# Attention ends shared out anew between VectorE and GpSimd, B's heads first in the output projection, and maxima that end a slot earlier, in a fused hybrid attention step

## The chip, the core and the metric

The kernel runs on one core of a Trainium2 chip. The metric is the device time of one execution in microseconds (us). The core's engines each run their own queue of instructions in order: TensorE (PE; its weight loads are PEld), VectorE (DVE), ScalarE (ACT), GpSimd (POOL) and SyncE (SP), which only issues DMAs here. They wait for one another by semaphores.

## What is computed

One layer of a diffusion backbone with two mixers, A (global attention, 8 query heads on 2 key heads) and B (attention in a window of 128 on either side, with a learned sink logit). There are 1024 latent tokens and 128 prompt tokens. Cut to what matters:

```python
h = rmsnorm(x, norm_gain) * (1.0 + scale) + shift           # adaLN
q_a, k_a, v_a, g_a, q_b, k_b, v_b, g_b = project(h, w_in)   # q and k normed, latents rotated
o_a = softmax(q_a @ [k_ctx, k_a].T / 8) @ [v_ctx, v_a]      # latents: all 9 blocks of 128 keys
o_b = softmax([sink, q_b @ [k_ctx, band(k_b)].T / 8])[1:] @ [v_ctx, band(v_b)]
x = x + gate * (concat(o_a * silu(g_a), o_b * silu(g_b)) @ w_out)
```

The prompt's tokens go through the same weights and attend to the prompt alone (one block of keys). All arithmetic is float32; products that need it are split into a high and a low part.

## The kernel before

The first 300 us make the modulation, the normed tokens, the projections (queries and gates go to DRAM, keys and values stay on the chip) and the gates. Then comes the attention, to which all of the change belongs.

**Units and slots.** A unit is (t, m, g): a tile t of 128 tokens, a mixer m (0 is A, 1 is B) and a group g of 4 heads. The units go t = 1 to 8, and for each t: A and B of group 0, then A and B of group 1; the prompt (t = 0) has the last four, units 32 to 35. A unit takes one slot for each of its key blocks: A 9, B 4 (3 for t = 1 and t = 8), a prompt unit 1, padded to 2. A pair of A and B thus has 13 slots. All engines' instructions are written out by one loop over slots, and the order that it gives is kept on each engine. A slot does this, in this order: what was put off to it by `later(n, f)` (f is run n slots on); the scores of its block (`scores`, st, and their exponentials pe); what `put` has entered for the slot in advance (maxima, B's weights); a share of the output projection from a queue `outq` (2 products a slot, 4 in the prompt); and, two slots after a unit's last block, its products with the values (`values`).

**A's softmax** uses a maximum over all keys, found beforehand: `max_items` makes 12 products pmx (L932) and as many reductions on VectorE (L933) in the 13 slots ahead of the unit. Its `finish` loads qb (the low part of the queries) and reduces the 12 maxima to m_nat (L943, L946); TURN slots later `transpose` lets TensorE turn m_nat to rows (ptm, L951) and VectorE multiply them into qb (L952), which the scores' second product (L1207) reads. `finish` stands at `start[i] - MX_LEAD` for latents and at `start[i] - LEAD` for the prompt; LEAD is 4 and does not change. Units 0 and 2 get theirs ahead of the loop, and for them, too, `transpose` comes TURN slots after `finish`.

**PSUM** is eight banks: A has two (pmx, ptm, B's first scores sn, and pti, a small transpose for B), B two (st), C two (pv, the products with the values), D and E one each (po, the output projection). A product that goes to a bank waits until its former content has been read.

**The end of a unit** (in `values`): T is the slot with the unit's last products. ENDS gives for A and B how many slots after T the steps come. For A: `inverse` at T+1 (ScalarE: rs, the reciprocals of the sums, as exp(-ln)), GpSimd's multiplication of the loaded gate sgl by rs at T+2 (L1248), `gated` at T+3 (VectorE: of = pv times sgl, L1254; it is written to the tile spare or of), `parts` at T+4 (ScalarE: the high part ogh, L1264) and T+5 (the low part ogl, L1267: GpSimd, or VectorE for units 30 and 31). B has its sums in earlier and steps at T+1 to T+4. At T+6 `out_items` puts the 24 products of the pair into `outq`: for each half of the columns, four 64-row pieces k of w_out in the order KS, and three products for each.

```python
MX_LEAD = 3
TURN = 2
ENDS = ((1, 3, 4), (1, 2, 3, 6))
KS = (0, 1, 4, 5, 2, 3, 6, 7)     # 0 to 3: A's heads, 4 to 7: B's; first four: group 0
```

On the prompt's last slots the scores of B are turned and normalised by VectorE (pen, L1030) before TensorE takes them (L1202); that needs the sums, which GpSimd completes (L1025).

Of the kernel before, what the change touches and what calls it, by code (L numbers as in the profile page):

```python
# [9 lines left out]
F32 = mybir.dt.float32  # L10
F32R = mybir.dt.float32r
BF16 = mybir.dt.bfloat16
AF = mybir.ActivationFunctionType
ALU = mybir.AluOpType
# [4 lines left out]
P = 128  # L19
# [12 lines left out]
CKV = {0: 512, 1: 1792}  # L32
WRAW = 3
PROMPT_AT = 32
KS = (0, 1, 4, 5, 2, 3, 6, 7)
PL_DVE = (4,)
LAG = 2
LEAD = 4
# [5 lines left out]
NAT_FIRST = (0, 1, 2, 3)  # L44
MX_AT = (-4, -3, -2, -2, -1, 4, 5, 5, 7, 7, 8, 8)
MX_FIRST = (0, 1, 2, 3, 3, 4, 4, 5, 6, 7, 7, 8)
MX_LEAD = 3
LAST_END = (1, 3, 5, 7)
SPLIT_LAG = 2

# [7 lines left out]
WO_LATE = {12: 9, 13: 10, 11: 21, 15: 21, 14: 24}  # L58

WO_STEPS = ((0, 4, 4), (1, 5, 5), (2, 6), (3, 7), (4, 8, 6), (5, 9), (6, 11), (7, 12, 10), (8, 12), (9, 13), (10, 14))  # L60
TURN = 2
QUERY_AT = (0, 2, 3, 6)
PAD = 2
X_FROM = 2
# [14 lines left out]
PES = 12  # L79
SPLIT = 6  # L80
GATE_LATE = 2
ENDS = ((1, 3, 4), (1, 2, 3, 6))
QTS = 5
PROMPT_LEAD = 4
PROMPT_PV = "CCAC"
# [45 lines left out]
def hybrid_step(ctx, tc, x_prompt, x_sample, cache_k_a, cache_v_a, cache_k_b, cache_v_b,  # L131
# [3 lines left out]
    nc = tc.nc  # L135
# [14 lines left out]
    def later(n, f):  # L150

        agenda.setdefault(now[0] + n, []).append(f)

    def tick():
        now[0] += 1
        for f in agenda.pop(now[0], ()):
            f()
# [8 lines left out]
    def bank(tag, name):  # L166
        return ps.tile([P, 512], F32, tag=tag, name=name, bufs=BANKS[tag])
# [174 lines left out]
    with tc.tile_pool(name="st", bufs=2, side="right") as st:  # L342
# [136 lines left out]
        for j in range(KT + 2):  # L479
# [79 lines left out]
            if KT - 2 <= j < KT:  # L559
# [3 lines left out]
                c0, n = W_QA.cols[0]  # L563
# [50 lines left out]
    with tc.tile_pool(name="qt", bufs=2, side="right") as qt:  # L614
# [108 lines left out]
        for m in range(2):  # L723
            w, nxt = ((W_QA, W_QB), (W_QB, W_KV))[m]
            ts = list(range(1, NT)) + [0]
            for t in ts:
# [3 lines left out]
                if (m, t) in ((0, ts[-2]), (1, ts[GATE_AT[0]])):  # L730
                    n = len(wg) // 2
# [171 lines left out]
    qtile, qbtile, mxtile, sgl = {}, {}, {}, {}  # L903
# [11 lines left out]
    def max_items(i):  # L915
# [19 lines left out]
        def finish():  # L935
# [10 lines left out]
            nc.vector.tensor_scalar(mn, m4, -1.0, None, op0=ALU.mult)  # L946
            later(TURN, transpose)

# [170 lines left out]
    for f in beside[2]:  # L1119
# [5 lines left out]
        name=nc.get_next_instruction_name(), engine=mybir.EngineType.Activation, act_func_set_id=6))  # L1125
# [3 lines left out]
    w2 = ctx.enter_context(tc.tile_pool(name="w2", bufs=2, side="right"))  # L1129
# [54 lines left out]
    def load_gate(i):  # L1184
        if i < NU:
            t, m, g = units[i]
            sgl[i] = w2.tile([P, 2, P], F32, tag="sgl", name=f"sgl{i}", bufs=4)
            h0 = HD * (8 * m + 4 * g)
            nc.sync.dma_start(
                sgl[i], g_dram[h0 : h0 + 4 * HD, P * place(t) : P * place(t) + P].rearrange("(c p) n -> p c n", p=P))  # L1190
# [27 lines left out]
    def values(i, made, first, last):  # L1218

        t, m, g = units[i]  # L1220
        if first:
            pvb[i] = bank("C", f"pv{i}")
        pv = pvb[i]

        def product(o, lhs, rhs, start, stop):
            r = rhs.rearrange("p (c s n) -> p c s n", s=2, n=P)
            for s in range(2):
                nc.tensor.matmul(pv[HD * s : HD * s + HD, o : o + 256].rearrange("p (c n) -> p c n", c=2), lhs,  # L1228
                                 r[:, :, s, :], start=start, stop=stop)

        n = len(made)
        for b, (blk, pe) in enumerate(made):
            product(0, blk[1], pe, first and b == 0, m == 1 and b == n - 1)
        if not last:
            return
        if m == 0:
            product(256, ones, acc.pop(i), False, True)

        v = {}

        def inverse():
            if m == 1:
                return
            rs = w2.tile([P, 256], F32, tag="rs", name=f"rs{i}")
            nc.scalar.activation(rs, pv[:, 256:512], AF.Ln)
            nc.scalar.activation(rs, rs, AF.Exp, scale=-1.0)
            sg = sgl[i]
            later(1, lambda: nc.gpsimd.tensor_tensor(sg, sg, rs.rearrange("p (c n) -> p c n", c=2), op=ALU.mult))  # L1248

        def gated():  # L1250
            o = 768 + 256 * (i % 4)
            of = spare[0][:, o : o + 256] if i % 4 < 3 else w2.tile([P, 256], F32, tag="of", name=f"of{i}", bufs=1)
            of = of.rearrange("p (c n) -> p c n", c=2)
            nc.vector.tensor_tensor(of, pv[:, 0:256].rearrange("p (c n) -> p c n", c=2), sgl.pop(i), op=ALU.mult)  # L1254
            later(GATE_LATE, lambda: load_gate(i + 4))
            v["of"] = of

        def parts():
            while held[0] == NOG:
                outq.pop(0)()  # L1260
            held[0] += 1
            oh = ogp.tile([P, 2, P], F32R, tag="ogh", name=f"ogh{i}")
            ol = ogp.tile([P, 2, P], F32R, tag="ogl", name=f"ogl{i}")
            nc.scalar.copy(oh, v["of"])  # L1264
            og[t, 2 * m + g] = oh, ol
            eng = nc.vector if i - PROMPT_AT in LOW_DVE else nc.gpsimd
            later(1, lambda: eng.tensor_tensor(ol, v["of"], oh, op=ALU.subtract))  # L1267

        for n, f in zip(ENDS[m], (inverse, gated, parts)):
            later(n, f)  # L1270
        if m == 1:
            later(ENDS[m][3], lambda: outq.extend(out_items(t, g)))

# [12 lines left out]
    def out_items(t, g):  # L1286

        last = t == units[-1][0]


        pieces = ((0, 512, "D"), (512, 768, "E"), (768, 1024, "C")) if last else ((0, 512, "D"), (512, 1024, "E"))

        def mm(c, k, p):

            a, b, tag = pieces[c]
            n = a // 512
            q = slice(a - 512 * n, b - 512 * n)
            if k == KS[0] and p == 0:
                po[c] = bank(tag, f"po{t}_{c}")[:, 0 : b - a]
            if c == 0 and k == KS[4] and p == 0:  # L1300
                for j in range(2):
                    load_sum(t, j)
            oh, ol = (x[:, k % 2, :] for x in og[t, k // 2])
            x, lo = ((oh, 0), (oh, 1), (ol, 0))[p]
            nc.tensor.matmul(po[c], x, wo_parts[KT * n + k][lo][:, q], start=(k == KS[0] and p == 0),  # L1305
                             stop=(k == KS[-1] and p == 2))
            if b == D and k % 2 == 1 and p == 2:
                held[0] -= 1
            if k == KS[-1] and p == 2:
                nc.vector.tensor_tensor(po[c], po[c], gt[n][:, q], op=ALU.mult)  # L1310
                nc.vector.tensor_tensor(yt[n][:, q], po[c], yt[n][:, q], op=ALU.add)
                nc.sync.dma_start(y_tile[t][:, a:b], yt[n][:, q])

        ks = KS[4 * g : 4 * g + 4]
        return [lambda c=c, k=k, p=p: mm(c, k, p) for c in range(len(pieces)) for k in ks for p in range(3)]
# [13 lines left out]
    for i, (t, m, g) in enumerate(units):  # L1329
        if i in EARLY:  # L1330
            continue
        if m == 0:
            items, done = max_items(i)
            at, end = [start[i - 2] + a for a in (MX_AT if i > 2 else MX_FIRST)], start[i] - MX_LEAD
            if t == 0:
# [19 lines left out]
    for i in range(4):  # L1355
        load_gate(i)
    for s in range(len(slots) + LAG + ENDS[1][3]):
        tick()
        if s < len(slots) and slots[s]:
            i, b, last, blk = slots[s]  # L1360
# [86 lines left out]
```

## Time and profile before

| | |
|---|---|
| time, median of 3 runs | 695.03 us (693.94 to 695.07) |
| the profiled execution | 694.89 us, its span 693.0 us |
| busy: TensorE, VectorE, GpSimd, ScalarE | 97%, 54%, 47%, 45% of the span |
| mean granted TensorE clock | 0.994 of full speed |
| 13 slots (a pair) in the middle of the attention | 22.7 us |

The span runs from the first to the last instruction; the rest of the execution's time lies around it. A row of the timeline gives the start, the duration, the engine, the source line, the operation, the tiles (written, then read), how many instructions the row joins, and in brackets how long the engine had been idle and what ended that. Of an engine that is busy 97% of the time, only its own idle time and what lengthens it count.

### The profile page before, as it was taken

The numbers are of one execution on the slowest core, as the hardware profiler recorded it, in microseconds if no ns is written. First come the engines' busy times: TensorE is split into PE (matmuls) and PEld (weight loads), VectorE is DVE, ScalarE is ACT, GpSimd is POOL, SyncE is SP. The second block draws the span as 40 slices with busy tenths as digits, with TensorE's granted clock in tenths as the row PEclk, the third lists the DMA queues.
The fourth block names the chain that finished last, engine by engine and source line by source line (L and its number), as shares of the span: only waits on it lengthen the run. The fifth ranks groups of instructions, "written<-read, shape, count | busy, mean of one in ns | idle before, by whom it ended". The sixth has DMA issues, their size and how long they took to land.

```text
span 693.0 us, 10923 instructions
## 1 busy us (share of the span) xinstructions
PE 675.0 (97%) x3896; PEld 522.8 (75%) x3896; DVE 374.3 (54%) x857; ACT 309.0 (45%) x692; POOL 323.3 (47%) x340
## 2 busy tenths in 40 slices
PE   6999999999999999998999999999999999999997
PEld 3688988878788788985667777777777777777666
DVE  3565237875684772535446455455455563645343
ACT  4555411412243452456445445555456445545450
POOL 3466023332322140657575457545664566446730
PEclk9999999999999999999899999999999999999999
DMA  8960283339436015533122122212221212112323
GB/s 339 413 255 21 109 303 77 78 92 285 133 88 191 8 62 161 165 105 108 58 82 71 54 85 68 92 54 69 70 84 47 91 61 78 55 55 68 122 61 122
DMA packets 53446, 78.65 MB, mean 113 GB/s; under 512 B 6848, under 2 KB 25728, under 8 KB 52368
## 3 DMA queue, kind: packets, MB, share of 16 engines
q1 hardware_dynamic: 45360, 66.28, 28.4%
q10 hardware_dynamic: 8032, 11.68, 6.3%
q8 instruction: 31, 0.51, 0.3%
q14 instruction: 23, 0.19, 0.1%
HBM read 58.72 MB, written 19.21 MB: 112 GB/s over the span
## 4 chain that ended last, share of the span: by engine, by line
PE 87%; DMA 4%; DVE 3%; ACT 2%; issue 1%; POOL 1%; ACTq 1%; SPq 1%; DVEq 0%; POOLq 0%
PE pv L1228 14%; PE po L1305 14%; PE st L1206 5%; PE pmx L932 5%; PE st L1207 4%; PE pq L279 4%; PE pq L280 4%; PE pq L278 4%; PE st L1202 4%; PE pg L288 3%; PE pg L292 3%; PE pg L293 3%; PE pk L279 2%; PE pk L280 2%; PE pk L278 2%; DMA wm<-in_w_mod_ss_dram 2%
## 5 line engine op out<-in xcount | busy, mean ns | idle before, releaser
L1215 POOL TENSOR_TENSOR acc<-acc,pe 128x512 f32<-128x512 f32 x112 | 143.5, 1281 | 37.8 <-ACT pe L1208 35.4
L933 DVE TENSOR_REDUCE mx<-pmx 128x1 f32<-128x384 f32 x192 | 101.7, 554 | 103.8 <-PE pmx L932 101.5
L1208 ACT ACTIVATE pe<-st 128x512 f32<-128x512 f32 x146 | 85.4, 596 | 89.8 <-PE st L1207 89.6
L1228 PE MATMUL pv<-pe,v_all 128*64 128x256 f32 x832 | 101.6, 387 | 0.0
L1228 PEld LDWEIGHTS pv<-pe,v_all 128*64 128x64 f32 x832 | 57.3, 138 | 38.3 <-issue 8.4
L993 DVE CUSTOM_DVE_ANT_0 sn<-sn,mask,nsink 128x512 f32<-128x512 f32 (+1 forms) x64 | 46.3, 724 | 68.6 <-PE sn L990 67.9
L1305 PE MATMUL po<-wo,ogh 128*128 128x512 f32 (+1 forms) x224 | 75.8, 390 | 0.0
L197 POOL TENSOR_TENSOR rs_q<-ms_q,mhalf 128x8 f32<-128x8 f32 x18 | 34.8, 1931 | 80.8 <-DVE ms_q L195 80.8
L932 PE MATMUL pmx<-kha,qt 128*128 128x384 f32 x192 | 63.3, 376 | 3.7 <-ACT pen L979 3.1
L1215 POOL TENSOR_TENSOR acc<-pe,pe 128x512 f32<-128x512 f32 x16 | 20.4, 1276 | 96.2 <-ACT pe L1208 73.9
L1206 PE MATMUL st<-qt,kha 128*128 128x512 f32 x144 | 61.4, 426 | 1.2 <-ACT pe L1208 1.1
L979 ACT ACTIVATE pen<-sn,nm 128x512 f32<-128x512 f32 (+2 forms) x72 | 45.3, 631 | 31.4 <-DVE nm L993 28.6
L1207 PE MATMUL st<-qb,kla 68*128 68x512 f32 x144 | 57.2, 397 | 0.0
L1203 ACT COPY pe<-st 128x512 f32<-128x512 f32 x62 | 36.4, 587 | 32.9 <-PE st L1202 32.9
L932 PEld LDWEIGHTS pmx<-kha,qt 128*128 128x128 f32 x192 | 34.9, 192 | 12.8 <-ACT pen L979 7.7
L1305 PEld LDWEIGHTS po<-wo,ogh 128*128 128x128 f32 x224 | 41.5, 190 | 3.5
L1305 PE MATMUL po<-wo,ogl 128*128 128x512 f32 (+1 forms) x112 | 43.6, 389 | 0.0
L1206 PEld LDWEIGHTS st<-qt,kha 128*128 128x128 f32 x144 | 27.2, 189 | 20.9 <-issue 8.5
L1202 PE MATMUL st<-ident_r,pen 128*128 128x128 f32 x248 | 37.5, 274 | 1.1 <-DVE pen L1030 1.1
L441 POOL TENSOR_TENSOR h<-hf,h 128x256 fp32r<-128x256 f32 (+2 forms) x33 | 28.0, 862 | 20.7 <-DVE h L440 20.7
L1202 PEld LDWEIGHTS st<-ident_r,pen 128*128 128x128 f32 x248 | 29.2, 141 | 7.5 <-ACT ogh L1264 1.5
L675 ACT ACTIVATE sqq<-pq 128x512 f32<-128x512 f32 x18 | 10.8, 599 | 53.3 <-DMA qd<-qo0q 15.6
(235 smaller groups left out, 1506.9 us busy)
## 6 DMA issues: line engine op xcount, KB each, us to landing
qt<-qd SPq DMA_DIRECT2D x36, 256.0 KB
wm<-in_w_mod_ss_dram SPq DMA_DIRECT2D x8, 1024.0 KB
qd<-qo0q ACTq DMA_DIRECT2D x36, 128.0 KB
qd<-qo1q ACTq DMA_DIRECT2D x36, 128.0 KB
sgl<-gd SPq DMA_DIRECT2D x36, 128.0 KB
out_dram<-yt SPq DMA_DIRECT2D x17, 256.0 KB
xn<-in_x_sample_dram SPq DMA_DIRECT2D x8, 512.0 KB
wg<-in_w_mod_g_dram SPq DMA_DIRECT2D x4, 1024.0 KB
```

The lines of the kernel that those rows point to most:

```text
L278: nc.tensor.matmul(out, h_at(0, i, k, tok), w.hi[k], start=(k == 0), stop=False)
L932: nc.tensor.matmul(pm[:, 0:384], lhs, kha[:, g, 3 * b : 3 * b + 3, :], start=True, stop=True)
L933: nc.vector.tensor_reduce(mx[:, h, b : b + 1], pm[:, 0:384], axis=AX.X, op=ALU.max)
L979: nc.scalar.activation(penat[i][:, h], s, AF.Exp, bias=v["nm"][:, h : h + 1], scale=scale, accum_out=v["sum"][:, h : h + 1])
L993: nc.vector.tensor_tensor_reduce(s, s, mask[:, m0 : m0 + n], -1.0, nsink[:, 4 * g + h : 4 * g + h + 1], op0=ALU.add, op1=ALU.min, accum_ou ...
L1202: nc.tensor.transpose(s[:, P * h : P * h + P], penat[i][:, h, o : o + P], ident_r.bitcast(F32))
L1206: nc.tensor.matmul(s, kh, qtile[i], start=True, stop=False)
L1207: nc.tensor.matmul(s, kl, qbtile[i], start=False, stop=True)
L1208: nc.scalar.activation(pe, s, AF.Exp)
L1215: nc.gpsimd.tensor_tensor(acc[i], first, pe, op=ALU.add)
L1228: nc.tensor.matmul(pv[HD * s : HD * s + HD, o : o + 256].rearrange("p (c n) -> p c n", c=2), lhs, r[:, :, s, :], start=start, stop=stop)
L1305: nc.tensor.matmul(po[c], x, wo_parts[KT * n + k][lo][:, q], start=(k == KS[0] and p == 0), stop=(k == KS[-1] and p == 2))
```

## The change

Five edits. (1) VectorE multiplies A's values by rs instead of by the gate, and GpSimd, right behind that in the same slot (T+3), multiplies the product by the gate; its multiplication at T+2 is gone. For B nothing changes. (2) `parts` for A comes at T+5 instead of T+4, so that the low part comes at T+6. (3) KS puts B's heads ahead of A's within each group. (4) MX_LEAD is 4 instead of 3: `finish` of a latent unit stands a slot earlier. (5) TURN is 3 instead of 2: `transpose` comes three slots after `finish`, so that it stays where it was for latents from unit 4 on, and comes one slot later for units 0 and 2 and for the prompt's units 32 and 34.

```diff
-KS = (0, 1, 4, 5, 2, 3, 6, 7)
+KS = (4, 5, 0, 1, 6, 7, 2, 3)
...
-MX_LEAD = 3
+MX_LEAD = 4
...
-TURN = 2
+TURN = 3
...
-ENDS = ((1, 3, 4), (1, 2, 3, 6))
+ENDS = ((1, 3, 5), (1, 2, 3, 6))
...
-            rs = w2.tile([P, 256], F32, tag="rs", name=f"rs{i}")
-            nc.scalar.activation(rs, pv[:, 256:512], AF.Ln)
-            nc.scalar.activation(rs, rs, AF.Exp, scale=-1.0)
-            sg = sgl[i]
-            later(1, lambda: nc.gpsimd.tensor_tensor(sg, sg, rs.rearrange("p (c n) -> p c n", c=2), op=ALU.mult))
+            v["rs"] = w2.tile([P, 256], F32, tag="rs", name=f"rs{i}")
+            nc.scalar.activation(v["rs"], pv[:, 256:512], AF.Ln)
+            nc.scalar.activation(v["rs"], v["rs"], AF.Exp, scale=-1.0)
...
-            nc.vector.tensor_tensor(of, pv[:, 0:256].rearrange("p (c n) -> p c n", c=2), sgl.pop(i), op=ALU.mult)
+            sg = sgl.pop(i)
+            by = sg if m else v["rs"].rearrange("p (c n) -> p c n", c=2)
+            nc.vector.tensor_tensor(of, pv[:, 0:256].rearrange("p (c n) -> p c n", c=2), by, op=ALU.mult)
+            if m == 0:
+                nc.gpsimd.tensor_tensor(of, of, sg, op=ALU.mult)
```

On TensorE, at the first two slots of the attention (st_0 and st_1 are unit 0's scores, sn_0 unit 1's; pg_late are products of the gates that are fitted in), there stands before:

```order
L951 MATMUL ptm_3392<-ident_r,m_nat_110 4x128
L1206 MATMUL st_0_3395<-qt_2991,kha 128x512
L1207 MATMUL st_0_3395<-qb_3181,kla 128x512
L989 MATMUL sn_0_3405<-khb,qt_2993 128x384
L990 MATMUL sn_0_3405<-klb,qt_2993 128x384
```

and after the change, from the last two of the six late products on:

```order
L1137 MATMUL pg_late<-h_2_0_140,late_ogl_2984 128x384
L1137 MATMUL pg_late<-h_2_0_142,late_ogh_2980 128x384
L951 MATMUL ptm_3412<-ident_r,m_nat_110 4x128
L1206 MATMUL st_1_3416<-qt_2991,kha 128x512
L1207 MATMUL st_1_3416<-qb_3181,kla 128x512
L989 MATMUL sn_1_3423<-khb,qt_2993 128x384
```

Unit 2's turn, ptm, has moved from ahead of slot 0 to ahead of slot 1, where sn_1 follows two products later; ptm and sn_1 have the same one of A's two banks, as they had before.

On TensorE in the prompt (pmx_0_0 is unit 34's, st_2 unit 31's, st_0 with khp unit 32's) stands before, around unit 34's maxima:

```order
L1305 MATMUL po_0_7118<-wo_4_3188,ogl_7061 128x512
L1305 MATMUL po_0_7118<-wo_5_3214,ogh_7060 128x512
L1202 MATMUL st_2_7200<-ident_r,pen_6982 128x128 x4
L929 MATMUL pmx_0_0_7210<-khp,qt_7103 128x128 x4
L1305 MATMUL po_0_7118<-wo_5_3215,ogh_7060 128x512
```

and after:

```order
L1307 MATMUL po_0_7118<-wo_0_3078,ogl_7090 128x512
L1307 MATMUL po_0_7118<-wo_1_3105,ogh_7089 128x512
L951 MATMUL ptm_7197<-ident_r,m_nat_109 4x128
L1202 MATMUL st_2_7200<-ident_r,pen_6982 128x128 x4
L929 MATMUL pmx_0_0_7210<-khp,qt_7102 128x128 x4
```

Unit 32's ptm now stands right ahead of unit 34's maxima, which go to the bank that ptm has; before, it stood 15 rows further up. In the same way unit 34's ptm now stands right ahead of unit 34's own scores (st_0 with qt_7102).

On VectorE and GpSimd a little later (nm is unit 35's maxima, of and spare the values of units 31 and 30, inv and pen unit 35's weights) VectorE has after the change:

```order
L1006 SCALAR_TENSOR_TENSOR nm_7262<-mx_7275,nsink 128x4
L952 TENSOR_TENSOR qb_7224<-ptm_7287,diag 4x512
L1254 TENSOR_TENSOR of_7290<-pv_7244,sgl_6855 128x256
L1254 TENSOR_TENSOR spare<-pv_7121,rs_7251 128x256
L1028 RECIPROCAL inv_7265<-sum_7263 128x4
L1030 TENSOR_TENSOR pen_7261<-pen_7261,inv_7265 128x512
```

where L952 stood two rows further up, ahead of unit 35's reduction, and GpSimd has, before and then after:

```order
L1248 TENSOR_TENSOR sgl_6875<-sgl_6875,rs_7254 128x256
L1011 TENSOR_TENSOR ex_7267<-nm_7265,sink 128x4
L1025 TENSOR_TENSOR sum_7266<-sum_7266,ex_7267 128x4
```

```order
L1011 TENSOR_TENSOR ex_7264<-nm_7262,sink 128x4
L1256 TENSOR_TENSOR spare<-spare,sgl_6875 128x256
L1025 TENSOR_TENSOR sum_7263<-sum_7263,ex_7264 128x4
```

The multiplication by the gate has moved to between unit 35's exponentials of the sink and its sums.

## The prediction

> **What bounds the kernel now.** I read the busy shares first, then the busy time by stretches, then TensorE's own list of waits.
>
> ```profile
> PE 675.0 (97%) x3896; PEld 522.8 (75%) x3896; DVE 374.3 (54%) x857; ACT 309.0 (45%) x692; POOL 323.3 (47%) x340
> 379.37:402.10 22.73, 22.72 (x138) 16.64 (x139) 11.68 (x29) 11.80 (x28) 13.21 (x15) 1.00 0.28 84
> PE pmx L932 <- ACT pen L979: 3.1, 3, 1.4
> ```
>
> TensorE is the bound: in a pair in the middle (13 slots, second row: length, busy TensorE, weight loads, VectorE, ScalarE, GpSimd) it is busy for 22.72 of 22.73 us, the others for 11.7 to 13.2. The change leaves TensorE's instructions as they are in number and shape. So it can win only what TensorE waits, and lose only by new waits. Of old ones in the attention the costliest entry is 3.1 us in three waits (third row), all in the first tiles. One more hides in busy time; the view of line 951 lists what its engine sat idle for, in us and times:
>
> ```profile
>   DVE mx L933: 5.8, 13
> ```
>
> Thirteen times the weight load of ptm stands until a reduction L933 is done. Here is one such place on both engines:
>
> ```profile
> 431.29 0.17 DVE L946 TENSOR_SCALAR m_nat<-m 128x4 fp32r<-128x4 f32 x1
> 432.89 1.02 DVE L933 TENSOR_REDUCE mx<-pmx 128x1 f32<-128x384 f32 x2 [0.52 <-PE pmx L932]
> 433.10 0.40 PE L1305 MATMUL po<-wo,ogh 128*128 128x512 f32 x1
> 433.51 0.22 PE L951 MATMUL ptm<-ident_r,m_nat 128*4 128x128 f32 x1
> ```
>
> m_nat is there at 431.46; ptm starts at 433.51, 0.06 us after the first of the two reductions can have ended (432.89 and half of 1.02, with an overlap: 433.45), since that frees ptm's bank. The product ahead of it started 0.41 us earlier; products of its kind follow each other by 0.23 us elsewhere (below, 667.04 and 667.27), so 0.18 us are lost.
>
> **The change part by part: the middle of the attention.** MX_LEAD 4 with TURN 3 brings m_nat a slot earlier and leaves ptm in place. As m_nat was never what ptm waited for, this wins nothing: 0. It puts L943 and L946 ahead of one reduction L933 instead of behind it:
>
> ```profile
> 430.31 0.17 DVE L1028 RECIPROCAL inv<-sum 128x4 f32<-128x4 f32 x1
> 430.62 0.56 DVE L933 TENSOR_REDUCE mx<-pmx 128x1 f32<-128x384 f32 x1
> 431.10 0.15 DVE L943 TENSOR_REDUCE m<-mx 128x4 f32<-128x12 f32 x1
> 431.36 0.42 PE L932 MATMUL pmx<-kha,qt 128*128 128x384 f32 x1
> ```
>
> That reduction frees the bank of the pmx at 431.36 and ends at 431.18. Between the reciprocal's end (430.48) and its start lie 0.14 us of idle VectorE, and the two small ones take 0.36 us from the first's start to the second's end. So it slips by up to 0.22 us, to 431.40, and with 0.06 us to TensorE the pmx by 0.10; with the overlap that VectorE's rows show (431.10 starts before 431.18) by less. I take 0 and keep 0.10 for 15 pairs, 1.5 us, as the upper end.
>
> The multiplications: VectorE's L1254 reads one PSUM and one SBUF operand of the same size as before, GpSimd's new one has the shapes of its old one. Their rows in one pair:
>
> ```profile
> 443.10 0.74 POOL L1248 TENSOR_TENSOR sgl<-sgl,rs 128x256 f32<-128x256 f32 x1
> 443.94 1.29 POOL L1215 TENSOR_TENSOR acc<-acc,pe 128x512 f32<-128x512 f32 x1
> 443.87 0.42 DVE L1254 TENSOR_TENSOR spare<-pv,sgl 128x256 f32<-128x256 f32 x1
> 445.13 0.42 ACT L1264 CAST ogh<-spare 128x256 fp32r<-128x256 f32 x1
> 445.43 0.62 ACT L1208 ACTIVATE pe<-st 128x512 f32<-128x512 f32 x1
> 446.88 0.20 ACT L1022 ACTIVATE ex<-ex 128x4 f32<-128x4 f32 x1 [0.83 <-POOL ex L1011]
> ```
>
> GpSimd now multiplies behind the sum that ends at 445.23; VectorE's product is there at 444.29, so the new wait holds nothing up. It ends at about 445.97. ScalarE's cast, which now waits for GpSimd, comes behind the exponential that ends at 446.05, into 0.83 us of idle time. Behind it in ScalarE's queue are exponentials for products a slot later. 0, with that 0.83 as cover. The cast and the low part come a slot later, but with B's heads first A's are read three slots later (six products at two a slot): 0. SP's load of the next gate now waits for GpSimd's read, which ends within the slot after T+3, and is issued at T+5: 0.
>
> **The start.** Unit 2's ptm moves from ahead of slot 0 to ahead of slot 1.
>
> ```profile
> 300.22 0.23 PE L951 MATMUL ptm<-ident_r,m_nat 128*4 128x128 f32 x1
> 300.48 0.68 DVE L952 TENSOR_TENSOR qb<-ptm,diag 4x512 fp32r<-4x512 f32 x1 [0.66 <-PE ptm L951]
> 302.19 0.39 PE L1206 MATMUL st<-qt,kha 128*128 128x512 f32 x1
> 302.65 0.34 PE L989 MATMUL sn<-khb,qt 128*128 128x384 f32 x1
> ```
>
> L952 starts 0.26 us after ptm and takes 0.68. ptm comes to about 302.13 (0.06 ahead of 302.19), so L952 ends at 303.07, and the sn at 302.65, which needs that bank, can start at 303.13: **+0.48 us**. Nothing behind takes it up, since the exponentials that follow wait for TensorE.
>
> **The prompt.** Unit 32's ptm moves to right ahead of unit 34's maxima (659.01), whose bank it has.
>
> ```profile
> 658.84 0.16 DVE L1006 SCALAR_TENSOR_TENSOR nm<-mx,nsink 128x4 f32<-128x4 f32 x1
> 658.66 0.60 PE L1202 MATMUL st<-ident_r,pen 128*128 128x128 f32 x4
> 659.01 0.65 PE L929 MATMUL pmx<-khp,qt 128*128 128x128 f32 x4
> ```
>
> ptm starts at 658.60, L952 at 658.92 (behind L1006), its end is 659.60 and L929 can start at 659.66: **+0.65 us**. Then unit 34's ptm stands ahead of the scores at 667.04:
>
> ```profile
> 667.04 0.39 PE L1206 MATMUL st<-qt,khp 128*128 128x512 f32 x1
> 667.27 0.40 PE L1207 MATMUL st<-qb,klp 68*128 68x512 f32 x1
> 667.07 0.42 DVE L1254 TENSOR_TENSOR of<-pv,sgl 128x256 f32<-128x256 f32 x1
> 667.40 0.42 DVE L1254 TENSOR_TENSOR spare<-pv,sgl 128x256 f32<-128x256 f32 x1
> 664.43 0.73 POOL L1248 TENSOR_TENSOR sgl<-sgl,rs 128x256 f32<-128x256 f32 x1 [2.25 <-ACT rs L1246]
> 668.93 0.20 POOL L1025 TENSOR_TENSOR sum<-sum,ex 128x4 f32<-128x4 f32 x1 [1.50 <-ACT ex L1022]
> 669.37 0.69 DVE L1030 TENSOR_TENSOR pen<-pen,inv 128x512 f32<-128x512 f32 x1
> 670.21 0.63 PE L1202 MATMUL st<-ident_r,pen 128*128 128x128 f32 x4 [1.06 <-DVE pen L1030]
> ```
>
> ptm at 666.98, L952 from 667.24 to 667.92; L1207 needs the qb that it writes and starts 0.15 us later (the step from L1030's end, 670.06, to 670.21), at 668.07 instead of 667.27: 0.80. But TensorE idles 1.06 us soon after, until 670.21, for pen. So what counts is how far pen slips: the two L1254 come behind L952 and end at 668.67, GpSimd's new multiplication (0.73) ends at about 669.45, and the sums, which stood at 668.93, come behind it: **+0.5 us** at 670.21, in which the 0.80 is contained. From there TensorE has products for the rest.
>
> **Near the end of tile 8** A's cast leaves its place between two exponentials:
>
> ```profile
> 647.51 0.59 ACT L1208 ACTIVATE pe<-st 128x512 f32<-128x512 f32 x1
> 647.99 0.40 ACT L1264 CAST ogh<-spare 128x256 fp32r<-128x256 f32 x1
> 648.28 0.61 ACT L1208 ACTIVATE pe<-st 128x512 f32<-128x512 f32 x1
> 648.49 0.39 PE L1207 MATMUL st<-qb,kla 68*128 68x512 f32 x1
> 648.94 0.19 PEld L1206 LDWEIGHTS st<-qt,kha 128*128 128x128 f32 x1 [0.50 <-ACT pe L1208]
> ```
>
> The second starts 0.29 us earlier, and the scores at 648.94, which need its bank, can come at 648.72 (0.23 behind 648.49): **-0.22 us**.
>
> **The sum.** 0.48 + 0.65 + 0.5 - 0.22 = 1.4 us. The profiled execution took 694.89 us (span 693.0), which gives 696.3; it lies 0.14 below the median of 695.03, from which I forecast **696.4**. Bounds: 0.7 where the start's stall is hidden, and 3.1 where the pairs lose 0.10 each and GpSimd's multiplication takes 0.2 more: 695.7 to 698.1. The bound of a measurement, 0.2%, is 1.4 us, so the forecast lies on it.
>
> **The rivals.** First, *the dip of the clock goes* (not slower).
>
> ```profile
> 325.70:332.60 6.90, 5.52 (x18) 3.87 (x20) 3.41 (x9) 3.65 (x9) 6.42 (x9) 0.58 0.56 184
> 327.08 1.01 PE L932 MATMUL pmx<-kha,qt 128*128 128x384 f32 x2 [1.38 <-ACT pen L979]
> ```
>
> For these 6.9 us the granted clock is 0.58, while 5.52 us of products run; at full clock they would take about half, 2.8 us less. The change puts a stall of 0.48 us ahead and shifts all behind it; if the dip then stays away, the time is 693.6. For it: the dip hangs on activity, as it begins in a wait. Against: the three times lie within 1.1 us, less than one dip, so it seems to come each time. The same mechanism is a rival on the slower side: *a dip in the prompt*, where the new waits stand close together. With 6.8 us at half clock in the last, gapless 18 us it costs 3.4: 699.8. It decides from where a wait is about as long as the 1.38 us of above; the new ones are each below 0.9, and the 1.06 us at 670.21 brought none. The Trainium skill, "TensorE: Matmul & The Clock Gate", Part 1, has the clock halved after at least one window of some 3.4 us of idleness. The trace does not agree: here it fell in a wait of 1.38 us. By that rule neither case could come, and the sum would stand at 696.4; I leave both a chance.
>
> Second, *the waits of ptm go*, because m_nat is earlier: 15 times 0.18 is 2.7 us, which gives 693.7. For it speaks the 5.8 us row; against it, that the row names L933, and that m_nat was 2 us early.
>
> Third, *the casts hold up ScalarE*: GpSimd is later than I think, the cast waits in front of exponentials, and the scores wait for their banks. With 0.3 us in 16 pairs, 4.8 us: 701.2. It begins where GpSimd is more than the 0.83 us later; GpSimd is busy for 13.2 of 22.7 us, so I hold it unlikely.
>
> **How the numbers follow.** Forecast 0.72, the dip gone 0.10, the waits of ptm gone 0.07, a dip in the prompt 0.07, ScalarE held up 0.04. Of the forecast's own range (695.7 to 698.1) about half lies beyond 696.4, the bound: 0.36 slower, 0.34 the same, 0.02 faster by the scatter of the runs. The two winning cases end at the other bound (693.6) and go half to faster, half to the same; the two last are slower. That makes faster 0.11, same 0.42, slower 0.47. The range reaches from 693.4, so that it takes in both winning cases, to 698.3, and leaves out the last two and the scatter.
>
> **What would show it.** In the profile after: a VectorE-ended wait of about 0.5 us before an sn at 303; one of 0.65 before L929 of the prompt; one before L1207 near 668.5; the wait for pen shorter, 0.7 to 0.8; pairs of 22.7 to 22.8 us, and 13 waits of ptm for L933 as before. I am wrong if a pair's length changes by over 0.1, if the waits at 303 and 659 are absent, or if the clock's row differs.

## The result and the profile after

The changed kernel takes **700.78 us** (median of 5, 700.39 to 700.92), the kernel before 694.87 (5 runs): ratio 1.0086, 95% interval 1.0071 to 1.0101. The forecast was 696.4 with a range up to 698.3: the sum pointed the right way, its size was wrong, and the time lies outside the range.

The page of the profile (its part on busy time) and the busy time by stretches, for a pair in the middle, show where it did not go and where it did:

```profile
PE 677.9 (97%) x3896; PEld 522.9 (75%) x3896; DVE 377.6 (54%) x857; ACT 309.9 (44%) x692; POOL 322.3 (46%) x340
388.80:411.99 23.19, 23.02 (x138) 16.76 (x137) 11.45 (x27) 11.92 (x28) 13.18 (x14) 1.00 0.21 64
```

The number of instructions is as before on every engine, and the bound is still TensorE; its busy time is 2.9 us longer and VectorE's 3.3. But a pair of units takes 23.19 us in place of 22.77 (the start of a pair's first scores to the next pair's, mean of 11 pairs; after 23.185, before 22.766). The prediction had named this as what would prove it wrong. TensorE's own waits in the attention (total, times, longest) that are new or have changed:

```profile
PE pmx L932 <- DVE mx L933: 2.4, 13, 0.5
PE st L1206 <- ACT pe L1208: 1.6, 2, 1.3
PE st L1202 <- DVE pen L1030: 0.7, 1, 0.7
PE pti L1040 <- DVE inv L1028: 0.5, 1, 0.5
PE st L1207 <- DVE qb L952: 0.5, 1, 0.5
PE pmx L929 <- DVE qb L952: 0.5, 1, 0.5
PE sn L989 <- DVE qb L952: 0.3, 1, 0.3
```

The first row is where the pairs lose; before it stood at 0.5 us, once. It shows only a part of the loss, since the modelled end of the product ahead hides the rest as busy time. The weight loads (PEld) of the same products show it better, first before, then after:

```profile
PEld pmx L932 <- DVE mx L933: 1.4, 3, 0.8
PEld pmx L932 <- DVE mx L933: 5.9, 14, 0.8
```

The place in one pair, after, in order of time; these are the rows that answer to the prediction's at 430.31 to 431.36:

```profile
429.97 1.28 POOL L1215 TENSOR_TENSOR acc<-acc,pe 128x512 f32<-128x512 f32 x1
430.35 0.17 DVE L1028 RECIPROCAL inv<-sum 128x4 f32<-128x4 f32 x1
430.46 0.17 DVE L943 TENSOR_REDUCE m<-mx 128x4 f32<-128x12 f32 x1
430.66 0.62 DVE L946 TENSOR_SCALAR m_nat<-m 128x4 fp32r<-128x4 f32 x1
431.19 0.54 DVE L933 TENSOR_REDUCE mx<-pmx 128x1 f32<-128x384 f32 x1
431.79 0.44 PE L932 MATMUL pmx<-kha,qt 128*128 128x384 f32 x1 [0.16 <-DVE mx L933]
```

L946 negates 4 numbers a partition. It took 0.17 us before and takes 0.62 now. (The reciprocal L1028 and the reduction L943 run beside the same sum and take 0.17 each; before, 0.17 and 0.15.) It starts at 430.66, while GpSimd adds exponentials (L1215, 429.97 to 431.25), and ends at 431.28 with that sum. The reduction L933 stands behind it and starts at 431.19 instead of 430.62, and the pmx that needs its bank comes at 431.79 instead of 431.36. The same sum ran at nearly the same time before:

```profile
429.94 1.28 POOL L1215 TENSOR_TENSOR acc<-acc,pe 128x512 f32<-128x512 f32 x1 [0.50 <-ACT pe L1208]
```

It ended at 431.22; L946 started at 431.29, just behind it. All places together, in the view of line 946 (shortest, median and longest in ns), first before, then after:

```profile
L946 DVE TENSOR_SCALAR m_nat<-m x16: 170/170/884, 284.3 to 635.1; 128x4 fp32r<-128x4 f32 x16
L946 DVE TENSOR_SCALAR m_nat<-m x16: 171/617/877, 283.8 to 638.8; 128x4 fp32r<-128x4 f32 x16
```

After, the negation starts inside a GpSimd instruction in 15 of these 16 places, and each time it ends 0.02 to 0.03 us behind it. The longest of before, 884 ns, was a hint that the prediction missed: it, too, started in the middle of a GpSimd instruction.

The difference of the two profiled executions, 698.6 - 693.0 = 5.6 us, by the start of the same product in each:

| place (time before) | us |
|---|---|
| ahead of the first scores (loads) | -0.57 |
| sn at 302.65 | +0.54 |
| 303 to 337 (mostly a shorter stretch of half clock) | -1.24 |
| 12 pairs, 337 to 617, 0.42 each | +5.07 |
| 617 to 638 (L946 again, there ahead of L1028: pti waits 0.5) | +0.50 |
| scores at 648.15 | +0.49 |
| scores at 648.94, to 650 | -0.30 |
| 650 to 659 | -0.20 |
| L929 at 659.01 | +0.72 |
| 667 to 670 | +0.60 |

### The profile page after: what moved, and what is told of

Same layout as the page of the kernel before. It is cut to its first block, busy times and chain, and to the rows that moved or that the text cites. A ratio compares the mean times of both kernels' runs of the same rounds, so it can differ in the third digit from the quotient of the medians.

```text
span 698.6 us, 10893 instructions
## 1 busy us (share of the span) xinstructions
PE 677.9 (97%) x3896; PEld 522.9 (75%) x3896; DVE 377.6 (54%) x857; ACT 309.9 (44%) x692; POOL 322.3 (46%) x340
## 4 chain that ended last, share of the span: by engine, by line
PE 83%; DVE 8%; DMA 4%; issue 2%; ACT 2%; POOL 1%; ACTq 1%; SPq 0%; DVEq 0%; POOLq 0%
PE pv L1228 14%; PE po L1307 12%; PE st L1206 5%; PE pmx L932 5%; PE st L1207 4%; PE pq L279 4%; PE pq L280 4%; PE pq L278 4%; PE pg L292 3%; PE pg L288 3%; PE pg L293 3%; DVE mx L933 3%; PE pk L279 2%; PE pk L280 2%; PE st L1202 2%; PE pk L278 2%
## 5 line engine op out<-in xcount | busy, mean ns | idle before, releaser
L1215 POOL TENSOR_TENSOR acc<-acc,pe 128x512 f32<-128x512 f32 x112 | 143.6, 1282 | 35.4 <-ACT pe L1208 33.8
L933 DVE TENSOR_REDUCE mx<-pmx 128x1 f32<-128x384 f32 x192 | 101.4, 552 | 104.2 <-PE pmx L932 103.7
L1208 ACT ACTIVATE pe<-st 128x512 f32<-128x512 f32 x146 | 83.2, 594 | 82.2 <-PE st L1207 82.1
L1215 POOL TENSOR_TENSOR acc<-pe,pe 128x512 f32<-128x512 f32 x16 | 20.4, 1275 | 102.0 <-ACT pe L1208 78.4
```

Of the source, the lines that this page charges most:

```text
L933: nc.vector.tensor_reduce(mx[:, h, b : b + 1], pm[:, 0:384], axis=AX.X, op=ALU.max)
L1208: nc.scalar.activation(pe, s, AF.Exp)
L1215: nc.gpsimd.tensor_tensor(acc[i], first, pe, op=ALU.add)
```

## The experiments

Theory A: the negation waits for a sum that runs on GpSimd, and the new place of the maxima puts it into one. Theory B: the new multiplication shifts GpSimd's queue. Theory C: any two small instructions ahead of L933 cost this. The kernel before, run beside them on the same chip, had a median of 693.8 to 694.1 us; ratios are against these runs.

**The maxima alone.**

```diff
--- before
-MX_LEAD = 3
+MX_LEAD = 4
-TURN = 2
+TURN = 3
```

> The kernel before with the maxima moved alone (MX_LEAD 4, TURN 3). Theory A (a wait of VectorE's negation L946 for GpSimd): in its new place the negation starts while a sum L1215 runs on GpSimd and ends only with it, 0.61 us instead of 0.17, in 13 or 14 units; the reduction L933 behind it and the pmx that waits for that reduction slip, and each pair of units takes 23.18 us instead of 22.76. With the two stalls of ptm at 303 and 659 (0.5 and 0.65 us) the time is about 694.9 + 5.5 + 1.2 = 701.6, between 700 and 702.5. Theory B (the new multiplications: GpSimd's queue shifts its sums, and these hold VectorE up): the move alone costs only the two stalls, 696.1, and L946 stays at 0.17.

Measured: 701.71 us, ratio 1.0110 (1.0097 to 1.0123). The view of line 946 and a pair's stretch:

```profile
L946 DVE TENSOR_SCALAR m_nat<-m x16: 169/616/878, 284.2 to 638.1; 128x4 fp32r<-128x4 f32 x16
388.90:412.10 23.20, 23.03 (x138) 16.72 (x137) 12.07 (x27) 11.84 (x28) 13.23 (x14) 1.00 0.18 54
```

The whole loss is here, without any of the new multiplications. Theory B is out.

**All but the maxima.**

```diff
--- after
-MX_LEAD = 4
+MX_LEAD = 3
-TURN = 3
+TURN = 2
```

> The changed kernel with the maxima where they were (MX_LEAD 3, TURN 2), so that the multiplications, the later parts of A and the order of the output products are left. Theory A: 694.9 within 0.6 (693.9 to 695.5), pairs of 22.76 us, L946 at 0.17 us. Theory B: the loss stays, about 700.

Measured: 692.59 us, ratio 0.9979 (0.9969 to 0.9988), pairs of 22.76 us. So the rest of the change is no loss but a gain of about 1 us (693.6 to 692.6 with the clock alike, in a table below). The lower end of the range expected was too high by 1.3. The cast that leaves its place near 648 gives 0.2 of it, as the prediction had it, and the scores at 627.47 come another 0.2 sooner; the remainder was not taken apart.

**Another kind of instruction in the same place.**

```diff
--- after
-        nc.gpsimd.tensor_copy(diag, ident[0:4, 0:4])
+        nc.gpsimd.tensor_scalar(diag, ident[0:4, 0:4], -1.0, None, op0=ALU.mult)
...
-            nc.vector.tensor_scalar(mn, m4, -1.0, None, op0=ALU.mult)
+            nc.vector.tensor_reduce(mn, m4.unsqueeze(2), axis=AX.X, op=ALU.max)
```

> The changed kernel with the negation L946 written as another kind of VectorE instruction in the same place: a reduction over one element that copies the maxima (the sign goes into diag), same tiles, same count. Theory A (it is this kind of instruction that waits for GpSimd): the copy takes about 0.17 us beside the running sum, pmx waits no more than 0.1, pairs of 22.76 to 22.86 us, time 700.8 less 13 times 0.42 = 695.3 (694.9 to 696.6). Theory C (any two small instructions ahead of L933 in that place cost this, by queue order or by a wait for m_nat's earlier reader): pairs stay at 23.18 us and the time at 700.8.

Measured: 694.92 us, ratio 1.0016 (1.0003 to 1.0028), pairs of 22.76 us. The place in the same pair, GpSimd and VectorE:

```profile
428.97 1.28 POOL L1215 TENSOR_TENSOR acc<-acc,pe 128x512 f32<-128x512 f32 x1
429.66 0.16 DVE L946 TENSOR_REDUCE m_nat<-m 128x4 fp32r<-128x4 f32 x1
429.74 0.55 DVE L933 TENSOR_REDUCE mx<-pmx 128x1 f32<-128x384 f32 x1
```

The copy runs in the middle of the sum and takes 0.16 us. With the same slot, the same count and the same tiles, 5.9 us are back. Theory C is out: the order of the queue costs next to nothing, as the prediction had it. It is the kind of instruction.

**The same instruction, behind the slot's own reduction.**

```diff
--- after
-        put(end, done)
+        ends.append((end, done))
...
+    for s, f in ends:
+        put(s, f)
```

> The changed kernel with L943 and L946 behind the slot's own reduction L933 and not ahead of it; the same slot, the same instructions, TURN 3. Theory A: the negation then starts about 0.6 us later, at the end of the sum L1215 or up to 0.2 us before it; it takes 0.17 to 0.35 us and no pmx waits for it: pairs of 22.76 us, 695.3 (694.7 to 696.5). If the place four slots ahead costs by itself, 700.8.

Measured: 695.38 us, ratio 1.0029 (1.0017 to 1.0041), pairs of 22.76 us.

```profile
428.73 1.28 POOL L1215 TENSOR_TENSOR acc<-acc,pe 128x512 f32<-128x512 f32 x1
430.08 0.17 DVE L946 TENSOR_SCALAR m_nat<-m 128x4 fp32r<-128x4 f32 x1
```

The sum ends at 430.01, the negation starts at 430.08 and takes 0.17. Four slots ahead is no trouble; 0.6 us within the slot are.

**A third kind: two operands in SBUF.**

```diff
--- after
+    nc.vector.memset(neg1, -1.0)
...
-            nc.vector.tensor_scalar(mn, m4, -1.0, None, op0=ALU.mult)
+            nc.vector.tensor_tensor(mn, m4, neg1[:, 0:4], op=ALU.mult)
```

> The changed kernel with the negation L946 as a product of two tiles in SBUF (the maxima and a tile of minus ones), same place, same size. Does this kind wait for GpSimd's sum as well? If the wait belongs to the form with one operand and a constant alone, it takes about 0.17 us and the time is that of the copy, 694.9 (693 to 697). If an instruction with two SBUF operands is held too, it takes about 0.61 us in 13 units, pairs of 23.18 us, and 700.8 (699.5 to 702).

Measured: 700.76 us, ratio 1.0104 (1.0088 to 1.0119), pairs of 23.19 us. Lines are one further on in this kernel:

```profile
428.74 2.70 POOL L1216 TENSOR_TENSOR acc<-acc,pe 128x512 f32<-128x512 f32 x2
430.86 0.61 DVE L947 TENSOR_TENSOR m_nat<-m,pad 128x4 fp32r<-128x4 f32 x1
```

It is held as long, to 431.47; the second of the two sums ends at 431.44. So two of three kinds wait for GpSimd and the reduction does not. The Trainium skill, "SBUF — State Buffer", section "Who interferes with whom", has a rule for this: VectorE's second pair of ports to SBUF (the memory that holds the tiles) is GpSimd's only one, and whichever issues first has it for a whole instruction; it is wanted by tensor_scalar (the negation's kind) in its two-port modes, and by kinds with two SBUF inputs beside a GpSimd instruction that reads SBUF, but on this chip never by a reduction. All three kinds agree with it (0.62, 0.61 and 0.16 us). That the negation ran in a two-port mode is not shown by itself.

**ptm two slots behind again, at the edges.**

```diff
--- after
-            later(TURN, transpose)
+            later(TURN if 2 < i < PROMPT_AT else 2, transpose)
```

> The changed kernel with ptm two slots behind the maxima again for unit 2 and for the prompt's units (TURN 3 stays for all others). If the three stalls are as the prediction priced them (0.48 at 303, 0.65 at 659, 0.5 at 670), the time is 700.8 - 1.6 = 699.2; the pairs stay at 23.18 us. If they were covered by something, 700.8. Of the 0.5 at 670 a part can stay, since GpSimd's new multiplication is still there: 699.2 to 699.7.

Measured: 699.02 us, ratio 1.0073 (1.0061 to 1.0085), pairs still 23.19 us. That is 1.76 us off, for 1.6 expected. Place by place in the two traces, the three stalls take 0.54, 0.70 and 0.55 us with them, so they cost about what they were priced at. The scores at 652.94 come 0.5 us sooner as well, which was not foreseen; with the clock alike (below) the gain is 2.0 us. The edit takes in unit 0 as well, whose ptm stands among the projections.

**Both remedies, and no negation at all.**

```diff
--- after
-                nc.vector.tensor_reduce(m4, mx, axis=AX.X, op=ALU.max)
...
-            nc.vector.tensor_scalar(mn, m4, -1.0, None, op0=ALU.mult)
-            later(TURN, transpose)
+                nc.vector.tensor_reduce(mn, mx, axis=AX.X, op=ALU.max)
...
+            later(TURN if 2 < i < PROMPT_AT else 2, transpose)
```

> The changed kernel without the negation L946 at all (the reduction L943 writes m_nat, the sign goes into diag) and with ptm two slots behind the maxima for unit 2 and the prompt. If theory A and the price of the three stalls both hold, nothing of the loss is left: 694.9 (the copy in place of the negation) less 1.6 = 693.3, from 692.3 to 694.3, by 0.2 to 1.5 us below the kernel before because of what is gained by the rest of the change. If a further loss sits in the new place of the maxima, it stays above 694.5.

Measured: 693.53 us, ratio 0.9998 (0.9989 to 1.0007). The held negation and the stalls together are nearly the whole loss; the time agrees with the sum expected to 0.2 us. But against the version with all but the maxima (692.59) 0.9 us is left, with the clock alike, too. A pair takes 22.79 us here and 22.76 there, which is 0.3 of it; the remainder was not taken apart.

**The wait of ptm, taken away for itself.**

```diff
--- before
-MX_AT = (-4, -3, -2, -2, -1, 4, 5, 5, 7, 7, 8, 8)
+MX_AT = (-4, -3, -3, -2, -1, 4, 5, 5, 7, 7, 8, 8)
```

> The kernel before with one of the two products pmx of the slot ahead of ptm a slot earlier (MX_AT -4, -3, -3, -2, -1), so that the reduction L933 that frees ptm's bank is done long before. The wait of ptm for L933 (5.8 us of idle weight loads, 13 times; by the prediction 0.18 us of TensorE each) goes: pairs of 22.58 us instead of 22.76 and 694.1 - 2.4 = 691.7. If another wait takes its place (the moved product for the bank of pti, freed by the copy L1044 on ScalarE, or the next pmx for its reduction), pairs stay within 0.05 us and the time at 694.

Measured: 691.31 us, ratio 0.9965 (0.9953 to 0.9977), pairs of 22.56 us. In the view of line 951 no wait for L933 is left:

```profile
its engine sat idle before it (us, times) until:
  issue: 0.4, 1
```

This was the prediction's second rival. It was worth what it was priced at, 0.2 us a pair; but the change does not touch it, since ptm waited for its bank and not for m_nat.

**That move on the changed kernel without its maxima.**

```diff
--- the kernel with all but the maxima
-MX_AT = (-4, -3, -2, -2, -1, 4, 5, 5, 7, 7, 8, 8)
+MX_AT = (-4, -3, -3, -2, -1, 4, 5, 5, 7, 7, 8, 8)
...
-            nc.vector.tensor_scalar(mn, m4, -1.0, None, op0=ALU.mult)
+                nc.vector.tensor_reduce(mn, mx, axis=AX.X, op=ALU.max)
```

> A version that is to beat both: the changed kernel with the maxima where they were (MX_LEAD 3, TURN 2, 692.6 so far), with the product pmx a slot earlier as above and without the negation. 692.6 - 2.4 = 690.2 if the waits of ptm go; 692.6 if they are replaced. The negation stands where no sum runs with MX_LEAD 3, so that its removal is worth no more than 0.2 us in all.

Measured: 692.71 us, ratio 0.9980 (0.9970 to 0.9990): a miss by 2.5 us, though the pairs are 22.57 us. The clock explains about half of it. Single executions of one kernel fall into three groups by their mean granted clock, according to whether TensorE ran no, one or two stretches of some 3.4 us at half clock (medians, with the number of executions; for the kernel before, those beside this run):

| kernel | clock 0.999 to 1.000 | 0.996 to 0.998 | 0.994, 0.995 |
|---|---|---|---|
| before | 692.19 (3) | 693.62 (20) | 694.86 (12) |
| after | | 700.78 (5) | |
| all but the maxima | 691.23 (1) | 692.59 (6) | 693.88 (1) |
| pmx a slot earlier | 690.27 (2) | 691.32 (8) | 693.55 (2) |
| the last one above | | 691.43 (5) | 692.96 (7) |

In one column the last one is 1.2 us below the kernel that it was made from, for 2.4 expected. It fell into two stretches more often, which is the other half of the miss. Where the first half is lost stays open: its products stand about 0.4 us later by 325, but so they did after the same move on the kernel before. Like for like, the changed kernel lost 7.2 us and not 5.9.

**The wait ahead of the half clock.** VectorE's L1254 of the first B unit waits 1.6 us for GpSimd's L1036, and TensorE 1.38 us behind it, in the tile where the clock falls.

```diff
--- before, with the product pmx a slot earlier
-        for n, f in zip(ENDS[m], (inverse, gated, parts)):
+        ends = (1, 3, 4, 7) if i in (1, 3) else ENDS[m]
+        for n, f in zip(ends, (inverse, gated, parts)):
...
-            later(ENDS[m][3], lambda: outq.extend(out_items(t, g)))
+            later(ends[3], lambda: outq.extend(out_items(t, g)))
```

> The kernel before with the product pmx a slot earlier (as in the run above, 691.3) and with the multiplication by the gate of the first two units of B (1 and 3), with what follows it, one slot later. VectorE waits there 1.6 us for GpSimd's product with the rows (L1254 for L1036), behind it the sums sn, ScalarE's pen and TensorE's pmx, which stood 1.38 us at 327 and at 352. If that queue is the cause, both waits shrink to below 0.4 us, 2 us in all, and with the wait at 327 the stretch of half clock behind it goes (1.2 us for one, 2.5 for two windows of it): 691.3 - 2 - 1.3 = 688, from 687 to 689.5. If pen is late for another reason, 691.3.

Measured: 691.24 us, ratio 0.9963 (0.9950 to 0.9977): a miss; nothing beyond the move of pmx. The rows at the place:

```profile
325.40 0.73 POOL L1248 TENSOR_TENSOR sgl<-sgl,rs 128x256 f32<-128x256 f32 x1
326.17 0.76 DVE L1254 TENSOR_TENSOR spare<-pv,sgl 128x256 f32<-128x256 f32 x2 [1.48 <-POOL sgl L1248]
327.45 0.65 PE L932 MATMUL pmx<-kha,qt 128*128 128x384 f32 x1 [1.32 <-DVE mx L933]
```

The wait at 327 was handed on: A's own L1254, next in the queue, wants the gate that GpSimd multiplies by rs right behind L1036. That at 352 shrank from 1.38 us to 0.33 and 0.57.

**The same on the changed multiplications.**

```diff
--- the kernel with all but the maxima
-MX_AT = (-4, -3, -2, -2, -1, 4, 5, 5, 7, 7, 8, 8)
+MX_AT = (-4, -3, -3, -2, -1, 4, 5, 5, 7, 7, 8, 8)
...
+        ends = (1, 3, 4, 7) if i in (1, 3) else ENDS[m]
...
```

> The changed kernel with the maxima where they were (MX_LEAD 3, TURN 2), and with both of those moves. The multiplications, the order of the heads and A's later parts then stand on the same ground as the run before; by the traces they are worth 0.5 to 1 us (the cast no longer between two exponentials near the end of tile 8): 687.3, from 686.3 to 688.8. If they are worth nothing, 688.

Measured: **687.97 us** (687.60 to 688.32), ratio 0.9914 (0.9901 to 0.9928), the fastest version here. All four executions have a clock of 1.000.

```profile
324.36 0.42 DVE L1254 TENSOR_TENSOR spare<-pv,rs 128x256 f32<-128x256 f32 x1
326.23 0.44 PE L932 MATMUL pmx<-kha,qt 128*128 128x384 f32 x1 [0.29 <-DVE mx L933]
```

Here VectorE multiplies by rs, which ScalarE has long made, and waits for nobody. TensorE's wait of 1.32 us is 0.29. So the changed multiplications do have a worth: they take GpSimd out of VectorE's way, and this shows only when the wait ahead of theirs is gone. The time lies between the two expected, but that is luck, since those built on a run of 688 that came out at 691.24. Against that run the multiplications, with A's later parts and the order of the heads, are worth 3.3 us, or 1.8 with the clock alike (687.97, and the single execution of 689.75 at 1.000): more than expected, and for another reason than the cast: TensorE's waits at 327 and 352 are together 1.6 us shorter than in that run.

## Why the prediction was wrong, by its steps

- *Start, +0.48*: right. Measured 0.54; the sn waits for qb.

```profile
302.62 0.44 PE L989 MATMUL sn<-khb,qt 128*128 128x384 f32 x1 [0.27 <-DVE qb L952]
```

- *Prompt, +0.65 and +0.5*: right. Measured 0.72 and 0.60, with the wait for pen at 0.72 as foreseen (0.7 to 0.8) and the sums behind GpSimd's new multiplication:

```profile
664.03 0.66 PE L929 MATMUL pmx<-khp,qt 128*128 128x128 f32 x4 [0.45 <-DVE qb L952]
673.06 0.50 PE L1207 MATMUL st<-qb,klp 68*128 68x512 f32 x1 [0.49 <-DVE qb L952]
673.87 0.73 POOL L1256 TENSOR_TENSOR spare<-spare,sgl 128x256 f32<-128x256 f32 x1 [1.42 <-DVE spare L1254]
674.56 0.20 POOL L1025 TENSOR_TENSOR sum<-sum,ex 128x4 f32<-128x4 f32 x1
675.85 0.63 PE L1202 MATMUL st<-ident_r,pen 128*128 128x128 f32 x4 [0.72 <-DVE pen L1030]
```

- *Tile 8's end, -0.22*: right (-0.30), but the scores at 648.15 came 0.49 later, which the prediction did not have. Their wait is 1.3 us instead of 0.9. It is 0.9 again in the version with the copy and in the one with ptm at two slots, and 1.3 in the ones with the maxima alone and with the negation behind the reduction. It starts at GpSimd's product with the rows of B's unit:

```profile
649.91 0.74 POOL L1036 TENSOR_TENSOR sgl<-sgl,spare 128x256 f32<-128x256 f32 x1 [0.43 <-ACT pe L1208]
```

The row names ScalarE, but what came last is the DMA of these rows (L1050): in the trace its last part lands at 649.77, 4.6 us after its issue. In the versions with 0.9 it lands 3.2 to 3.6 us after the issue, and GpSimd does not wait for it. What makes the DMA slower stays open.
- *The middle, 0 with 0.10 as the upper end*: **this step failed.** The chain was the right one, L943 and L946 ahead of one L933, its bank, the pmx. The term was mis-sized: the two were put at 0.36 us by rows in which the negation starts just behind GpSimd's sum (431.29 against 431.22), and measured 0.82 (430.46 to 431.28), because the negation now starts inside that sum and is held until it ends. That makes 0.42 us a pair instead of 0 to 0.10, 5.1 us in 12 pairs. The section counted what the moved instructions queue behind and who queues behind them on VectorE; it did not ask what runs on GpSimd at the new time.
- *The sum's bounds*: the lower one, 0.7 us, is 0.9 by its own terms (1.4 less 0.48). Nothing hangs on it: the upper one had 0.10 us a pair where 0.42 was measured.
- *The multiplications, 0*: no loss, right; the gain that they hold was not seen.
- *The rivals*: the waits of ptm stayed, as argued. In the changed kernel the half clock came for one stretch of some 3.4 us instead of two (the row's window lies inside it):

```profile
328.40:331.70 3.30, 3.30 (x13) 2.12 (x13) 1.26 (x3) 1.18 (x3) 3.30 (x6) 0.52 0.79 220
```

A dip in the prompt did not come here, though the wait at 652.94 was 1.34 us. It did come with the maxima alone, behind a wait of 1.39 us, the length from which the prediction had let it begin; it was 3.4 us long and not 6.8:

```profile
652.33 0.50 PE L1206 MATMUL st<-qt,kha 128*128 128x512 f32 x1 [1.39 <-ACT pe L1208]
654.40:657.70 3.30, 3.30 (x16) 1.54 (x16) 1.54 (x3) 0.66 (x2) 3.30 (x5) 0.51 0.73 217
```

## What to carry to other kernels

When an instruction moves, take its price at the new time and not from its old row: look at what the other engine of a shared resource runs there, and read the longest duration in its group beside the median. A few numbers on VectorE can cost as much as the GpSimd instruction that they run into; here a reduction in their place, or the same multiplication 0.6 us later, cost next to nothing. A wait that is taken away may be handed to the next instruction in the queue, so read what that one wants.

## What the runs showed of the hardware

- A VectorE multiplication of 128x4 in SBUF, by a constant or by a tile, that starts beside GpSimd's 128x512 sum ends with that sum: 0.61 us against 0.17. A reduction of the same size in the same place takes 0.16, and the reciprocal of 128x4 that runs beside the same sum 0.17.
- Stretches of half clock last some 3.4 us or twice that, and one kernel has none, one or two of them from execution to execution, at 1.0 to 2.2 us each by the table above. In the traces each one between products began in a wait of TensorE of 1.3 to 1.4 us or within 2 us behind one. But such a wait is not enough: the one at 350 to 353 us stands in eleven traces, and none has a stretch there. With the waits of 1.3 us gone from the first tiles of the attention, none was left in four executions.
